# Unit phases of a diagonal state-space scan: a doubling ladder on VectorE, or products of two small tables on GpSimd

## The chip, the cores and the metric

The kernel runs on one core of a Trainium2 chip. Its time is the time of one execution in microseconds (us), as the device counts it; a kernel's figure is the median of several executions. The profile is of one such execution. Engines are named as in the profile: PE is TensorE's matmul, PEld its weight load, DVE is VectorE, ACT is ScalarE, POOL is GpSimd, and SP is SyncE, which only issues DMAs here. A semaphore orders the engines among each other; on one engine, instructions run strictly in the order of the program.

## The reference, cut to what matters

One decoder layer over 512 tokens of width 2048. An input projection gives 24 blocks of 128 channels: 8 go into a diagonal state-space group (S5), 16 into a gated causal convolution of 31 taps. Both are joined, go through an output projection and a layer norm, then through a mixture of 32 experts, and a last gated embedding.

```python
z = x @ w_in + b_in
lam_bar = exp(lam * exp(log_dt))              # complex, 64 groups x 64 states
bu = einsum('blgh,gph->blgp', u, b_bar)
states = scan(s[t] = lam_bar * s[t-1] + bu[t])
y = einsum('blgp,ghp->blgh', states, c).real + d_skip * u
...
h = conv31(v * sigmoid(g)); y_conv = silu(layer_norm(h))
y = concatenate([y_ssm, y_conv]) @ w_o + b_o
```

The kernel splits the 512 steps into 64 columns of 8 steps. Over the columns it needs a complex scan with the factor lam_bar^8. It takes the angle out: the input of column n is turned back by the unit phase exp(-i a n), a real scan with the modulus runs over the columns, and the result is turned forward by exp(i a n). So it needs, for each of the 64 groups and 64 states, cos(a n) and sin(a n) for n = 0 to 63. Those are the unit phases.

## The kernel before, in words

Stage 1 goes over the 24 blocks of the input projection in the order written in `order` (lines 268 and 594 to 629). A block is 48 matmuls of 128x512 into the bank `zp` (`mm3`, lines 99 to 102: each product is split in a high and a low part, three matmuls). Their weights come as `raw` over SP, ACT casts the high part `whi` (line 79), and DVE, for the last four blocks and for the GLU weights POOL, takes the low part `wlo` (line 80). Between the matmuls of later blocks stand the small matmuls of the state-space tiles: `x_mm` (L516), `y_mm` (L540 and L541), the transposes L466 and the kernel products L473 and L474.

For each of the 8 state-space blocks (tiles), `ssm_tables(ft)` makes what depends on parameters alone. On POOL: `bw` (L439 to L444) and the tables `wt` and `t1` (L452 to L454). On ACT: the copies `wx`, `kpad`, `mt`, and eight copies that spread the phases `cc` and `ss` into `pc` and `pz` (L495 to L498). `bw` has one buffer, so POOL's L439 of a tile waits until PE has read the tile before (L474); `cc` and `ss` have one buffer too, so they are written again only after ACT's eight copies. `ssm_tile` then does the scan on DVE: L525 to L534, with the scan itself at L529; its result `sc` goes to `y_mm`. `activate` takes the bank `yp` with an ACT copy (L548), sends it through DRAM, and DVE and ACT apply the skip and the GELU (L553 to L560); SP writes the result to `z_dram` (L561).

The phases are made by `phases(ft)`, once for two tiles: a ladder of six doublings, n = 1, 2, 4, 8, 16, 32, each of six DVE instructions (L412 to L417) on 128 x 8 x n elements, 36 instructions a call and four calls. POOL only sets the first element (L404, L405).

Each convolution channel block is 30 DVE instructions in a row (L236, "taps"), with the running sum in a PSUM bank `cps`; their result `acc` goes to `c_dram` over SP (L238). DVE has no other large work that is as free to wait: blocks 0 to 5 of the convolution end with the tap loop inside stage 1.

Stage 2 begins when all eight `z_dram` are back in SBUF as `zraw` (L608) and split into `zh` and `zl`: four blocks of GLU matmuls (192 of 128x512), then the output projection, first with the state-space half `y0`, later with the convolution half `y1`. Its DVE work is the last taps, the GLU gate (L717), the low parts `y0l`, and additions of the bias (L741). The mean over channels of the convolution is taken on PE by L686 and L687, after DVE's L677. Stage 3 routes the tokens and streams expert weights, stage 4 is the gated embedding.

The order on each engine isn't the order of the source: a scheduler plays the program through with its own estimate of durations and writes the engines' instructions in the order in which they would start. A change of one instruction's engine so moves others too.

Of the kernel before, what the change touches and what calls it, by code (L numbers as in the profile page):

```python
# [8 lines left out]
FT = mybir.dt.float32  # L9
# [3 lines left out]
OP = mybir.AluOpType  # L13
# [4 lines left out]
P = 128  # L18
# [4 lines left out]
NN = S // NB  # L23
# [31 lines left out]
def build(tc, I, out, dbg=None, stages=9):  # L55
    nc = tc.nc
    V = nc.vector
    A = nc.scalar
    G = nc.gpsimd
# [72 lines left out]
    def exp_parts(pool, x, shape, tag):  # L132
        def w(nm, dt=FT):
            return pool.tile(shape, dt, name=f"{tag}{nm}")
        xc, k, r, h, k2 = w("xc"), w("k"), w("r"), w("h"), w("k2")
        s = w("s", I32)
        V.tensor_scalar(xc, x, -87.0, 88.0, op0=OP.max, op1=OP.min)
        V.tensor_scalar(k, xc, LOG2E, MAGIC, op0=OP.mult, op1=OP.add)
        V.tensor_scalar(k, k, -MAGIC, None, op0=OP.add)
        V.scalar_tensor_tensor(r, k, -LN2H, xc, op0=OP.mult, op1=OP.add)  # L140
        V.scalar_tensor_tensor(r, k, -LN2L, r, op0=OP.mult, op1=OP.add)
        V.tensor_scalar(h, r, 1.0 / 5040, None, op0=OP.mult)
        for cf in (1.0 / 720, 1.0 / 120, 1.0 / 24, 1.0 / 6, 0.5, 1.0):
            V.scalar_tensor_tensor(h, h, cf, r, op0=OP.add, op1=OP.mult)
        V.tensor_scalar(k2, k, 127.0, 8388608.0, op0=OP.add, op1=OP.mult)
        V.tensor_copy(s, k2)
        return h, s.bitcast(FT)
# [96 lines left out]
    def bank(name, bufs=1):  # L244
        if name in bturn:

            n = bturn[name]
            bturn[name] += 1
            name, bufs = (("zp", 4) if n % 5 < 4 else ("xp", 1)) if name == "ops" else (("wps", "cps")[n % 2], 1)
        return psA.tile([P, 512], FT, name=name, tag=name, bufs=bufs)  # L250

    if True:
        with ExitStack() as s2:
            xpool = s2.enter_context(tc.tile_pool(reuse_waits="tile", name="xpool", bufs=1))
            vstk = ExitStack()
            tpool = vstk.enter_context(tc.tile_pool(reuse_waits="tile", name="tpool", bufs=1))
# [38 lines left out]
            spool = setup.enter_context(tc.tile_pool(reuse_waits="tile", name="spool", bufs=1))  # L295
# [10 lines left out]
            h, s2k = exp_parts(spool, ldt, [P, 1, NG], "edt")  # L306
# [13 lines left out]
            h, s2k = exp_parts(spool, er, [P, 2, NG], "eer")  # L320
# [67 lines left out]
                V.tensor_tensor(hi, hi, t4, op=OP.add)  # L388
            V.tensor_scalar(Li, Li, sig, None, op0=OP.mult)

            Cb = tpool.tile([P, 8, 4, 6], FT, name="Cb")
            Sb = tpool.tile([P, 8, 4, 6], FT, name="Sb")
            for dst, srct in ((Cb, cs), (Sb, sn)):
                for hf in range(2):
                    ph = slice(64 * hf, 64 * hf + 64)
                    V.tensor_copy(dst[ph].rearrange("p t g j -> p j t g"),
                                  srct[ph, 1:7].rearrange("p j (t u g) -> p j t u g", t=8, u=2)[:, :, :, hf])

            def phases(ft):

                cc = tpool.tile([P, 8, NN], FT, name="cc")
                ss = tpool.tile([P, 8, NN], FT, name="ss")
                tm = vpool.tile([P, 8, NN // 2], FT, name="tm", tag="xr", bufs=1)
                G.memset(cc[:, :, 0:1], 1.0)  # L404
                G.memset(ss[:, :, 0:1], 0.0)  # L405
                bases = [t[:, ft:ft + 2].rearrange("p t g j -> p (t g) j") for t in (Cb, Sb)]
                for j in range(6):
                    m = 1 << j
                    cb_, sb_ = (b[:, :, j:j + 1].broadcast_to([P, 8, m]) for b in bases)
                    t_ = tm[:, :, 0:m]  # L410
                    c0, c1, s0, s1_ = cc[:, :, 0:m], cc[:, :, m:2 * m], ss[:, :, 0:m], ss[:, :, m:2 * m]
                    V.tensor_tensor(c1, c0, cb_, op=OP.mult)  # L412
                    V.tensor_tensor(t_, s0, sb_, op=OP.mult)
                    V.tensor_tensor(c1, c1, t_, op=OP.subtract)
                    V.tensor_tensor(s1_, s0, cb_, op=OP.mult)
                    V.tensor_tensor(t_, c0, sb_, op=OP.mult)
                    V.tensor_tensor(s1_, s1_, t_, op=OP.add)  # L417
                return cc, ss

            cs_pair = []  # L420
            setup.close()
            vpool = vstk.enter_context(tc.tile_pool(reuse_waits="tile", name="vpool", bufs=2))
            E = G

            def ssm_tables(ft):
# [20 lines left out]
                big = tpool.tile([P, GT, CH, NB], FT, name="big")  # L446
# [23 lines left out]
                for g in range(GT):  # L470
                    j, c = g % 4, g // 4
# [15 lines left out]

                pc = vpool.tile([P, GT, NN], FT, name="pc", bufs=2)
                pz = vpool.tile([P, GT, NN], FT, name="pz", bufs=2)
                if ft % 2 == 0:  # L490
                    cs_pair[:] = phases(ft)
                cc, ss = (t[:, 4 * (ft % 2):4 * (ft % 2) + 4] for t in cs_pair)
                for hf in range(2):
                    src_, gh = slice(64 * hf, 64 * hf + 64), slice(4 * hf, 4 * hf + 4)
                    A.copy(pc[0:64, gh], cc[src_])  # L495
# [98 lines left out]
            for s_, f in enumerate(order):  # L594
# [18 lines left out]
                kind, j = f // 8, f % 8  # L613
                if s_ == 2:
                    tabs[0] = ssm_tables(0)
                if kind == 0:
                    u = vpool.tile([P, S], FT, name="u", bufs=3)
                    A.activation(u, ps, AF.Identity, bias=b_in[:, j:j + 1])
                    ssm_tile(j, u, tabs.pop(j))
                    if j < 7:  # L620
                        tabs[j + 1] = ssm_tables(j + 1)
                elif kind == 1:
                    gates[j] = ps
                else:
                    hcs.append(conv_gate(j, gates.pop(j), ps))
                    if 1 <= j < 7:
                        conv_taps(j - 1)
                    if j == 6:
                        conv_taps(6)
# [4 lines left out]
    if True:  # L634
# [59 lines left out]
        sh = [P, NT, P]  # L694
        rows = []
        for x, n in ((rs4, "sqs"), (d4, "near")):
            t = lp_.tile(sh, FT, name="diag", tag=n)
# [5 lines left out]
        sh_ = lp_.tile([P, S], FT, name="sh_")  # L703
        A.copy(sh_, ps)

        for q in range(4):
            hl = next(w_in)
            for f in range(2):
                wh, wl = hl[f]
                ps = bank("ops")  # L710
                for k in range(8):
                    sl = slice(k * P, (k + 1) * P)
                    mm3(ps, wh[:, sl], wl[:, sl], zh[:, k], zl[:, k], k == 0, k == 7)
                ft = 2 * q + f
# [66 lines left out]
        with ExitStack() as s3:  # L781
# [126 lines left out]
            def rt(name, *shape):  # L908
                return rp.tile([P, *shape], FT, name=name)
# [38 lines left out]
            cn, cc = bank("ops"), bank("ops")  # L948
# [25 lines left out]
            sv = rt("sv", 3, 2 * NT)  # L974
# [62 lines left out]
    if True:  # L1037
# [105 lines left out]
        for i, (width, members) in enumerate(GROUPS):  # L1143
# [16 lines left out]
            with tc.If(most > 0):  # L1160
                cv, cg = Carve(ob), Carve(gx)
                sv, place = cv.tile([P, 3, 2 * NT]), cv.tile([P, NP])
# [56 lines left out]
    with ExitStack() as s5:  # L1219
# [111 lines left out]
        for c in range(4):  # L1331
# [18 lines left out]
            for m in range(NT):  # L1350
# [14 lines left out]
                if c == 3:  # L1365
                    gate(m, c, ps[m], bpg)
                    mean, rstd = ln_stats(fh, st3[:, m], "s")
                    for q in range(2):
                        i = slice(q * 1024, (q + 1) * 1024)
# [67 lines left out]
```

## Time and profile before

| | us |
|---|---|
| median of 3 runs | 1529.64 (1523.28 to 1530.3) |
| the profiled execution | 1528.31 |
| its span, first to last instruction | 1526.6 |
| stage 1, to the first GLU matmul | 0 to 418.2 |
| GLU and output projection | 418 to about 700 |
| routing | about 700 to 785 |
| experts | 785 to about 1280 |
| gated embedding | to the end |

In the whole span PE is busy 83%, DVE 54%, ACT 24%, POOL 22%. The shares mean little for this change: in stage 1 DVE is busy nearly all the time, later hardly. In the expert stage the chain that ended last is nearly all DMA of expert weights, each piece a load of some 20 us. The stages follow each other: the expert weights that are routed can't be asked for before the routing is done.

### The profile page before, as it was taken

What the parts mean: (1) busy time and instruction counts of PE and PEld (TensorE: products, weight loads), DVE (VectorE), ACT (ScalarE), POOL (GpSimd) and SP (SyncE); (2) the same over time, 40 slices, a digit from 0 to 9 for tenths busy, and PEclk for the clock granted to TensorE, in tenths of its full rate; (3) what the DMA queues carried; (4) which work ended last, traced back from release to release, by engine and by line L of the source; (5) the groups of instructions that cost most, each with busy time, mean ns of one, the idle gap of its engine ahead of it and who ended that gap; (6) DMA issues with size and microseconds to landing.
All of it is one profiled execution on the core that took longest, in us unless ns stands there. A gap on an engine that the chain in (4) does not pass through costs nothing. (4 is left out here: it accounts for less than half of the span.)

```text
span 1526.6 us, 16736 instructions
## 1 busy us (share of the span) xinstructions
PE 1260.8 (83%) x6206; PEld 806.8 (53%) x6207; DVE 825.5 (54%) x1369; ACT 371.6 (24%) x558; POOL 332.8 (22%) x273
## 2 busy tenths in 40 slices
PE   6988989899489999997639898977776766489996
PEld 4766768777368788874313332312211211378884
DVE  7999999969998934375101111100000005976567
ACT  4332634454243613122000111100000003023210
POOL 0444435373283520000001111100000003710000
PEclk9989889999799999998669999998889887689998
DMA  6333434433723235123899999999999996326312
GB/s 227 109 99 116 132 112 136 123 113 110 273 102 123 77 114 200 58 81 151 344 407 387 420 412 420 421 417 417 416 410 410 420 398 245 117 109 228 120 60 117
DMA packets 97497, 349.21 MB, mean 229 GB/s; under 512 B 29688, under 2 KB 43256, under 8 KB 61824
## 3 DMA queue, kind: packets, MB, share of 16 engines
q1 hardware_dynamic: 50880, 303.08, 51.2%
q10 hardware_dynamic: 40912, 28.20, 6.3%
q0 software_dynamic: 5616, 16.79, 2.8%
q8 instruction: 51, 0.84, 0.2%
q14 instruction: 38, 0.31, 0.1%
HBM read 323.17 MB, written 35.34 MB: 235 GB/s over the span
## 5 line engine op out<-in xcount | busy, mean ns | idle before, releaser
L1093 PE MATMUL gu<-ring,xt 128*32 128x512 f32 (+2 forms) x1144 | 234.8, 676 | 54.3 <-DMA ring<-w_gu 54.2
L236 DVE SCALAR_TENSOR_TENSOR cps<-hc,wdw,cps 128x512 f32<-128x512 f32 x232 | 174.0, 750 | 3.2
L100 PE MATMUL zp<-xh,whi 128*128 128x512 f32 x384 | 157.7, 412 | 10.7 <-ACT whi L79 10.1
L79 ACT CAST whi<-raw 128x1024 fp32r<-128x1024 f32 x116 | 119.4, 1046 | 177.6 <-PE zp L102 60.0
L1093 PEld LDWEIGHTS gu<-ring,xt 128*32 128x32 f32 (+2 forms) x1144 | 58.8, 128 | 194.7 <-issue 102.9
L102 PE MATMUL zp<-xh,wlo 128*128 128x512 f32 x384 | 156.0, 406 | 3.1 <-DVE wlo L80 3.1
L101 PE MATMUL zp<-xl,whi 128*128 128x512 f32 x384 | 156.5, 408 | 1.6 <-DVE xl L80 1.6
L80 DVE TENSOR_TENSOR wlo<-raw,whi 128x1024 fp32r<-128x1024 f32 x90 | 119.3, 1336 | 59.8 <-ACT whi L79 58.8
L1099 DVE TENSOR_TENSOR act<-act,gu 128x256 f32<-128x256 f32 x13 | 5.5, 422 | 259.1 <-ACT act L1098 259.1
L1113 PE MATMUL dps<-ring,at 128*32 128x512 f32 (+2 forms) x568 | 116.7, 625 | 10.7 <-ACT at L1104 5.5
L1063 POOL DMA_INDIRECT y_dram<-ob,sl x26 | 25.6, 986 | 364.7 <-ACT ob L1115 355.5
L100 PE MATMUL fps<-whi,h2h 128*128 128x512 f32 x224 | 89.6, 401 | 1.0 <-ACT h2h L79 1.0
L102 PE MATMUL fps<-whi,h2l 128*128 128x512 f32 x224 | 89.7, 401 | 0.0
L100 PEld LDWEIGHTS zp<-xh,whi 128*128 128x128 f32 x384 | 75.2, 196 | 26.2 <-ACT whi L79 9.8
L101 PE MATMUL fps<-wlo,h2h 128*128 128x512 f32 x224 | 88.9, 398 | 0.0
L1078 DVE COPY xt<-xtp 128x512 f32<-128x512 f32 x26 | 18.0, 692 | 128.5 <-PE xtp L1073 128.5
L102 PEld LDWEIGHTS zp<-xh,wlo 128*128 128x128 f32 x384 | 75.2, 196 | 20.9 <-DVE wlo L80 4.3
L80 POOL TENSOR_TENSOR wlo<-raw,whi 128x1024 fp32r<-128x1024 f32 x26 | 68.0, 2621 | 81.1 <-ACT whi L79 72.6
L101 PEld LDWEIGHTS zp<-xl,whi 128*128 128x128 f32 x384 | 75.3, 196 | 17.4 <-DVE xl L80 2.0
L1115 DVE COPY ob<-dps 128x512 f32<-128x512 f32 x26 | 18.0, 692 | 103.5 <-PE dps L1113 103.5
L1113 PEld LDWEIGHTS dps<-ring,at 128*32 128x32 f32 (+2 forms) x568 | 31.5, 122 | 79.6 <-issue 57.7
L1073 PE MATMUL xtp<-ident,gx 128*128 128x128 f32 x208 | 35.9, 298 | 39.1 <-DMA gx<-h_dram,sl 29.7
(434 smaller groups left out, 2287.1 us busy)
## 6 DMA issues: line engine op xcount, KB each, us to landing
ring<-w_gu SPq DMA_DIRECT2D x114, 1024.0 KB, 20.9
ring<-w_dn SPq DMA_DIRECT2D x56, 1024.0 KB, 20.6
raw<-w_in SPq DMA_DIRECT2D x24, 1024.0 KB, 5.5
raw<-w_o SPq DMA_DIRECT2D x16, 1024.0 KB, 4.8
raw<-w_gu SPq DMA_DIRECT2D x14, 1024.0 KB, 19.0
raw<-w_pg SPq DMA_DIRECT2D x14, 1024.0 KB, 5.8
raw<-w_dn SPq DMA_DIRECT2D x8, 1024.0 KB, 23.9
raw<-y_dram SPq DMA_DIRECT2D x12, 512.0 KB, 6.8
```

Source lines behind the costliest of these rows:

```text
L79: A.copy(hi, src)
L80: eng.tensor_tensor(lo, src, hi.bitcast(FT), op=OP.subtract)
L100: T.matmul(ps, lh, rh, start=start, stop=False)
L101: T.matmul(ps, lh, rl, start=False, stop=False)
L102: T.matmul(ps, ll, rh, start=False, stop=stop)
L236: V.scalar_tensor_tensor(ps if k < 30 else acc, hc[:, k:k + S], wdw[:, ct, k:k + 1], ps, op0=OP.mult, op1=OP.add)
L1063: G.indirect_dma_start(out=y_dram[q], out_offset=bass.IndirectOffsetOnAxis(ap=isc, axis=0), in_=ob[:, q * 1024:(q + 1) * 1024], in_offset= ...
L1073: T.transpose(ps[:, kk * P:(kk + 1) * P], gx[:, k * P:(k + 1) * P], ident)
L1078: V.tensor_copy(o, ps)
L1093: T.matmul(gu[cols], xt[:, k, cols], raws[j][:, kk * 512:(kk + 1) * 512], start=k == 0, stop=k == KD - 1)
L1113: T.matmul(outs[c][cols], at[:, k, cols], raws[j][:, o:o + 512], start=k == 0, stop=k == 1)
L1115: (A.copy if c else V.tensor_copy)(ob[:, q * 1024 + c * 512:q * 1024 + (c + 1) * 512], outs[c])
```

## The change

`phases` goes. The table of powers is made once for all tiles on DVE: `tc_` and `ts_` hold cos and sin of 8 low powers (n = 0 to 7) and of 8 high ones (n = 0, 8, ..., 56), for all 32 rows of groups, by three doublings of six instructions each, 18 instructions in all. In each of the 8 tiles POOL then makes `cc` and `ss` as the product of high and low power: six instructions of 128 x 256 elements, with a piece of `big` as scratch. `cc` and `ss` now cover one tile instead of two, still with one buffer each.

```diff
@@ -388,36 +388,32 @@
                 V.tensor_tensor(hi, hi, t4, op=OP.add)
             V.tensor_scalar(Li, Li, sig, None, op0=OP.mult)
 
-            Cb = tpool.tile([P, 8, 4, 6], FT, name="Cb")
-            Sb = tpool.tile([P, 8, 4, 6], FT, name="Sb")
+            Cb = spool.tile([P, 8, 4, 6], FT, name="Cb")
+            Sb = spool.tile([P, 8, 4, 6], FT, name="Sb")
             for dst, srct in ((Cb, cs), (Sb, sn)):
                 for hf in range(2):
                     ph = slice(64 * hf, 64 * hf + 64)
                     V.tensor_copy(dst[ph].rearrange("p t g j -> p j t g"),
                                   srct[ph, 1:7].rearrange("p j (t u g) -> p j t u g", t=8, u=2)[:, :, :, hf])
 
-            def phases(ft):
-
-                cc = tpool.tile([P, 8, NN], FT, name="cc")
-                ss = tpool.tile([P, 8, NN], FT, name="ss")
-                tm = vpool.tile([P, 8, NN // 2], FT, name="tm", tag="xr", bufs=1)
-                G.memset(cc[:, :, 0:1], 1.0)
-                G.memset(ss[:, :, 0:1], 0.0)
-                bases = [t[:, ft:ft + 2].rearrange("p t g j -> p (t g) j") for t in (Cb, Sb)]
-                for j in range(6):
-                    m = 1 << j
-                    cb_, sb_ = (b[:, :, j:j + 1].broadcast_to([P, 8, m]) for b in bases)
-                    t_ = tm[:, :, 0:m]
-                    c0, c1, s0, s1_ = cc[:, :, 0:m], cc[:, :, m:2 * m], ss[:, :, 0:m], ss[:, :, m:2 * m]
-                    V.tensor_tensor(c1, c0, cb_, op=OP.mult)
-                    V.tensor_tensor(t_, s0, sb_, op=OP.mult)
-                    V.tensor_tensor(c1, c1, t_, op=OP.subtract)
-                    V.tensor_tensor(s1_, s0, cb_, op=OP.mult)
-                    V.tensor_tensor(t_, c0, sb_, op=OP.mult)
-                    V.tensor_tensor(s1_, s1_, t_, op=OP.add)
-                return cc, ss
-
-            cs_pair = []
+
+            tc_, ts_ = (tpool.tile([P, 2, 32, 8], FT, name=n) for n in ("tc_", "ts_"))
+            V.memset(tc_[:, :, :, 0:1], 1.0)
+            V.memset(ts_[:, :, :, 0:1], 0.0)
+            tm_ = spool.tile([P, 2, 32, 4], FT, name="tm_")
+            bases = [t.rearrange("p t g (a j) -> p a (t g) j", a=2) for t in (Cb, Sb)]
+            for j in range(3):
+                m = 1 << j
+                cb_, sb_ = (b[:, :, :, j:j + 1].broadcast_to([P, 2, 32, m]) for b in bases)
+                t_ = tm_[:, :, :, 0:m]
+                c0, c1, s0, s1_ = (t[:, :, :, a:a + m] for t in (tc_, ts_) for a in (0, m))
+                V.tensor_tensor(c1, c0, cb_, op=OP.mult)
+                V.tensor_tensor(t_, s0, sb_, op=OP.mult)
+                V.tensor_tensor(c1, c1, t_, op=OP.subtract)
+                V.tensor_tensor(s1_, s0, cb_, op=OP.mult)
+                V.tensor_tensor(t_, c0, sb_, op=OP.mult)
+                V.tensor_tensor(s1_, s1_, t_, op=OP.add)
+
             setup.close()
             vpool = vstk.enter_context(tc.tile_pool(reuse_waits="tile", name="vpool", bufs=2))
             E = G
@@ -487,9 +483,17 @@
 
                 pc = vpool.tile([P, GT, NN], FT, name="pc", bufs=2)
                 pz = vpool.tile([P, GT, NN], FT, name="pz", bufs=2)
-                if ft % 2 == 0:
-                    cs_pair[:] = phases(ft)
-                cc, ss = (t[:, 4 * (ft % 2):4 * (ft % 2) + 4] for t in cs_pair)
+                cc, ss = (tpool.tile([P, 4, NN], FT, name=n) for n in ("cc", "ss"))
+                sh = [P, 4, 8, 8]
+                cl, ch, sl, sh_ = (t[:, a, 4 * ft:4 * ft + 4].unsqueeze(3 if a else 2).broadcast_to(sh) for t in (tc_, ts_) for a in range(2))
+                cv, sv = (t.rearrange("p g (a b) -> p g a b", b=8) for t in (cc, ss))
+                tm = big.rearrange("p g h i -> p (g h i)")[:, 0:256].rearrange("p (g a b) -> p g a b", a=8, b=8)
+                E.tensor_tensor(cv, ch, cl, op=OP.mult)
+                E.tensor_tensor(tm, sh_, sl, op=OP.mult)
+                E.tensor_tensor(cv, cv, tm, op=OP.subtract)
+                E.tensor_tensor(sv, sh_, cl, op=OP.mult)
+                E.tensor_tensor(tm, ch, sl, op=OP.mult)
+                E.tensor_tensor(sv, sv, tm, op=OP.add)
                 for hf in range(2):
                     src_, gh = slice(64 * hf, 64 * hf + 64), slice(4 * hf, 4 * hf + 4)
                     A.copy(pc[0:64, gh], cc[src_])
```

The scheduler moves much else. Three places follow. The first is POOL from the end of tile 0's tables to the start of tile 1's. Before:

```order
L453 TENSOR_TENSOR big<-Li,cb 128x1024
L454 TENSOR_TENSOR t_510<-t_510,big 128x1024
L404 MEMSET cc 128x8
L569 MEMSET hc 128x30
L439 TENSOR_TENSOR bw<-ba,qr 128x8x16
```

and now:

```order
L449 TENSOR_TENSOR big<-Li,cb 128x1024
L450 TENSOR_TENSOR t_533<-t_533,big 128x1024
L492 TENSOR_TENSOR big<-ts__308 128x256
L493 TENSOR_TENSOR cc<-cc,big 128x256
L495 TENSOR_TENSOR big<-tc__307,ts__308 128x256
L496 TENSOR_TENSOR ss<-ss,big 128x256
L491 TENSOR_TENSOR cc<-tc__307 128x256
L494 TENSOR_TENSOR ss<-ts__308,tc__307 128x256
L573 MEMSET hc 128x30
L435 TENSOR_TENSOR bw<-ba,qr 128x8x16
```

The phases of a tile stand behind its tables, the first two instructions of the next tile's phases right behind them, and then `bw` of the next tile. L491 and L494 wait for ACT's copies of the tile before.

The second place is SP at the end of stage 1 (`z_dram_78` to `85` are the eight tiles' results, `c_dram_86` to `92` those of convolution blocks 0 to 6). Before:

```order
L75 DMA raw<-w_glu 128x2048
L561 DMA z_dram_85<-gl 128x512
L238 DMA c_dram_92<-acc 128x512
L608 DMA zraw<-z_dram_78 128x512
...
L608 DMA zraw<-z_dram_85 128x512
L611 DMA hcv<-c_dram_86 128x512
```

and now:

```order
L238 DMA c_dram_91<-acc 128x512
L565 DMA z_dram_85<-gl 128x512
L612 DMA zraw<-z_dram_78 128x512
...
L612 DMA zraw<-z_dram_85 128x512
L615 DMA hcv<-c_dram_86 128x512
...
L75 DMA raw<-w_o 128x2048
L238 DMA c_dram_92<-acc 128x512
L615 DMA hcv<-c_dram_92 128x512
```

The write of convolution block 6 stood ahead of the loads of `zraw`, and now stands behind them.

The third place is DVE at the same point. Before:

```order
L236 SCALAR_TENSOR_TENSOR cps<-hc,wdw,cps 128x512 x12
L236 SCALAR_TENSOR_TENSOR acc<-hc,wdw,cps 128x512
L234 TENSOR_SCALAR cps<-hc,wdw,bdw 128x512
L236 SCALAR_TENSOR_TENSOR cps<-hc,wdw,cps 128x512 x6
L80 TENSOR_TENSOR zl<-zraw,zh 128x512
```

and now:

```order
L236 SCALAR_TENSOR_TENSOR acc<-hc,wdw,cps 128x512
L562 TENSOR_TENSOR gl<-gl,yc 128x512
L234 TENSOR_SCALAR cps<-hc,wdw,bdw 128x512
L236 SCALAR_TENSOR_TENSOR cps<-hc,wdw,cps 128x512
L564 TENSOR_TENSOR gl<-yc,gl 128x512
L236 SCALAR_TENSOR_TENSOR cps<-hc,wdw,cps 128x512 x7
L80 TENSOR_TENSOR zl<-zraw,zh 128x512
```

The `acc` in the first piece is that of convolution block 6, in the second that of block 5: with the change, 8 taps of block 6 stand ahead of `zl`, and 22 of it and all 30 of block 7 behind it.

## Rows read from the trace of the kernel before

**Rows 1.** Windows: us, each engine's busy us (instructions), TensorE clock, DMA share, GB/s.

```profile
30.00:418.00 388.00, 332.09 (x1803) 272.28 (x1801) 367.36 (x541) 164.46 (x254) 170.72 (x135) 0.92 0.43 134
390.00:420.00 30.00, 8.39 (x33) 6.23 (x31) 27.55 (x39) 6.36 (x10) 5.15 (x5) 0.67 0.78 292
418.00:506.00 88.00, 83.43 (x350) 65.99 (x351) 81.72 (x115) 35.27 (x58) 51.50 (x29) 0.95 0.33 114
```

**Rows 2.** Waits of PE, 0 to 700 us: us in total, times, longest.

```profile
PE zp L100 <- ACT zh L79: 21.6, 1, 21.6
PE yp L540 <- ACT yb L548: 12.4, 3, 7.4
PE xp L516 <- ACT whi L79: 7.5, 1, 7.5
PE yp L541 <- DVE sc L534: 5.9, 2, 5.5
PE wps L466 <- POOL wt L454: 4.9, 1, 4.9
```

**Rows 3.** Timeline of SP, end of stage 1: start us, us, engine, line, what.

```profile
404.24 0.33 SPq L561 DMA_DIRECT2D z_dram<-gl  x1
414.40 0.33 SPq L238 DMA_DIRECT2D c_dram<-acc  x1
414.77 3.94 SPq L608 DMA_DIRECT2D zraw<-z_dram  x8
```

**Rows 4.** Timeline of PE: last tile's L541, end of stage 1, one in stage 2.

```profile
386.31 0.39 PE L541 MATMUL yp<-sc,t 128*128 128x63 f32 x2
...
396.21 0.40 PE L102 MATMUL zp<-xh,wlo 128*128 128x512 f32 x1
...
505.69 0.39 PE L101 MATMUL zp<-wlo,y0h 128*128 128x512 f32 x1
```

**Rows 5.** DVE groups, 0 to 418 us: count | busy us, mean ns | idle before.

```profile
L414 DVE TENSOR_TENSOR cc<-cc,tm 128x8 f32<-128x8 f32 (+5 forms) x24 | 17.4, 723 | 0.0
L413 DVE TENSOR_TENSOR tm<-ss,Sb 128x8 f32<-128x8 f32 (+5 forms) x24 | 16.3, 677 | 0.1
L416 DVE TENSOR_TENSOR tm<-cc,Sb 128x8 f32<-128x8 f32 (+5 forms) x24 | 14.7, 613 | 0.2
L412 DVE TENSOR_TENSOR cc<-cc,Cb 128x8 f32<-128x8 f32 (+5 forms) x24 | 11.0, 460 | 0.0
L417 DVE TENSOR_TENSOR ss<-ss,tm 128x8 f32<-128x8 f32 (+5 forms) x24 | 10.1, 419 | 0.0
L415 DVE TENSOR_TENSOR ss<-ss,Cb 128x8 f32<-128x8 f32 (+5 forms) x24 | 7.8, 323 | 0.0
L383 DVE TENSOR_TENSOR Lr<-Lr 128x64 f32<-128x64 f32 (+2 forms) x3 | 1.0, 337 | 0.0
```

**Rows 6.** Timeline of DVE and of POOL, 285 to 288 us.

```profile
285.72 1.70 DVE L413 TENSOR_TENSOR tm<-ss,Sb 128x8 f32<-128x8 f32 x1
287.34 0.74 DVE L236 SCALAR_TENSOR_TENSOR cps<-hc,wdw,cps 128x512 f32<-128x512 f32 x1
...
285.37 2.03 POOL L452 TENSOR_TENSOR wt<-Lr,bw 128x1024 f32<-128x1024 f32 x1
```

**Rows 7.** POOL groups of the nearest sizes, 0 to 560 us.

```profile
L443 POOL TENSOR_TENSOR sm<-ba,qi 128x128 f32<-128x128 f32 x8 | 4.8, 601 | 0.4
L670 POOL TENSOR_TENSOR near<-near,hcv 128x512 f32<-128x512 f32 x4 | 5.8, 1458 | 0.3
```

**Rows 8.** Timeline of ACT: one of the eight copies.

```profile
154.06 0.41 ACT L498 ACTIVATE pz<-ss 64x256 f32<-64x256 f32 x1
```

**Rows 9.** Waits of POOL, 0 to 560 us: us in total, times, longest.

```profile
POOL bw L439 <- PE wps L474: 45.1, 6, 15.9
POOL cc L404 <- ACT pc L496: 23.0, 1, 23.0
```

**Rows 10.** DVE groups, 418 to 506 us.

```profile
L766 DVE TENSOR_TENSOR hcv<-hcv,cps 128x512 f32<-128x512 f32 x8 | 4.9, 676 | 0.0
```

## The prediction, made before the changed kernel ran

> **What bounds the kernel now.** I read the busy shares by slice first: DVE is full in the first third of the span and nearly empty in the middle, and the removed work lies in that first third. So stage 1 is looked at alone. Its windows [rows 1] show DVE busy 367 of the 388 us from 30 to 418, 95%, and POOL 171, under half; PE looks busy at 332, but matmuls overlap, and its waits tell more. In stage 1 four groups hold it up, together 12.4 + 7.5 + 5.9 + 4.9 = 30.7 us, and one wait of 21.6 us ends the stage [rows 2]. Behind such waits the clock falls: the window's mean granted clock is 0.92, so 0.08 x 388 = 31 us of full speed are missing [rows 1]. Some 10 of them fall into the last wait (0.33 x 30 in the window 390 to 420 [rows 1]); of the rest I put 5 inside the other waits and 16 on matmuls that ran at the lower level. So PE loses 31 + 16 + 22 = 69 us to the other engines in stage 1, and could have reached the GLU at about 418 - 69 = 349.
>
> DVE's figure is alike. Almost without a gap it has done 418 us of its order when the stage ends. Both engines so have about the same bound, once DVE has less to do. PE's waits are mostly for DVE, directly or in a chain: ACT takes its instructions in order and waits for DVE, and PE for ACT.
>
> The last wait is worth a look [rows 3, 4]. PE ends its last block at 396.2 + 0.4. The last tile's result goes out at 404.2, and its reload is the next thing that PE needs; but SP has the write of convolution block 6 in between, whose taps DVE finishes only at 414.4. The reload starts at 414.8, PE at 418.2.
>
> **The change, part by part.**
>
> Removed from DVE: six groups of 24 instructions, 17.4 + 16.3 + 14.7 + 11.0 + 10.1 + 7.8 = 77.3 us [rows 5]. That is much for so little data, and rows 6 show why: an instruction on 128x8 elements takes 1.70 us, from 285.72 to 287.42, and POOL's L452 runs from 285.37 to 287.40. A DVE instruction with both inputs in SBUF waits until POOL's is through. A tap right behind it, with one input in PSUM, takes its 0.74 us [rows 6].
>
> The Trainium skill, SBUF — State Buffer, section "SBUF: two separate sides", states that as a rule: one port pair is an exclusive lock between a DVE instruction with two SBUF inputs and a GpSimd instruction, the later one blocks for the whole of the other. The trace agrees (1.70 us). Perfetto Trace Analysis, section "Optimizing Scalar/DVE Operations", in the Trainium skill draws the conclusion that moving work between the two might not help. It is the third rival below.
>
> Added on DVE: 18 instructions on up to 128x256 elements at the 0.337 us of L383 [rows 5], 6 us, early, where DVE also waits for loads. Bounds: 3 and 12 us.
>
> Added on POOL: 48 instructions on 128x256. Between 0.60 us for 128x128 and 1.46 for 128x512 [rows 7] I take 0.8, as a straight line gives: 38 us, and keep 29 and 70 as ends. What covers them: POOL waits 45.1 us, six times, for PE before it may write `bw` again [rows 9], 7.5 us a tile. Four of the six stand just ahead of that wait, and so do the next tile's first two. The latter wait in their turn for ACT's copies; I put 1.7 us on that (four copies are left after `ss`, 0.41 each [rows 8]). 6 x 0.8 + 1.7 = 6.5, under 7.5, though not by much. The wait of 23.0 us [rows 9] was the same kind: POOL stood before a memset of `cc`, until ACT had the phases from DVE, and the tables of tile 1, for which PE waits 4.9 us, were behind it. POOL now makes these phases itself right after tile 0's tables, and I expect this wait to go.
>
> The price on DVE: 38 us more of POOL in which its remaining two-input instructions may be caught. Bounds 0 and 38. The taps aren't caught and fill about half of DVE's time; I take 5. So DVE is relieved by 77 - 6 - 5 = 66 us in stage 1.
>
> What that gives. If PE lost no time, the GLU would start at 349 plus 3 or so, that is 66 earlier; DVE, at 418 - 66, and with 22 taps x 0.74 = 16 us [rows 6] moved behind the stage, would be ready at 336. I don't take it whole: some of PE's waits are for transfers and for ACT's own order, and two engines that are both near their bound hold each other up. Of the 31 + 16 us I count half, 24 us. The last wait I count as gone but for 3: SP no longer has block 6 in front of the reload, and the y matmuls of the last tile stand 2.2 blocks (some 25 us) before the end of the projection, where 22 us are needed from them to the GLU (386.3 to 404.2, and from 414.8 to 418.2 for the reload [rows 3, 4]). That is 19 us. Together 43.
>
> What is late next. The 22 taps, 16 us, now lie behind `zl`, before the subtraction for which L687 waits and partly before `y0l` of the last GLU block, which PE needs. DVE was busy 81.7 of 88 us from 418 to 506 [rows 1]. Of that some 14 us (L766 with 4.9 [rows 10], and the small steps of the norm and some additions) now come later, and 16 come in: 84 us of work, 87 to 92 us with its gaps. PE's matching point, the 311th large matmul of stage 2, was at 505.7 [rows 4], 87.5 us after 418.2. So PE gives back 0 to 5 us there and once more clock; I take 4. From there on PE is busy without a gap until about 700, the order of the later engines is nearly the old one, and routing and experts follow: what is left is kept to the end.
>
> Sum: 43 - 4 = 39 us. Against the profiled execution 1528.3 - 39 = 1489; that lies 1.3 us under the median of the runs, so 1490 for a median.
>
> **The rivals.**
>
> *All waits go.* DVE was the one cause. For it: its 95%, and that each of the four waits leads back to a late DVE or POOL result. Against: two bounds that meet at 336 to 352. Gain 66 - 4 = 62: 1468 as a median, like the times below.
>
> *DVE only filled its time.* The taps may wait for long, so less DVE work only brings them forward, and PE's waits, of which two name ACT, stay. Only the reload's 19 us are won, less 4: 1515.
>
> *The lock takes half of it back.* All 38 us of POOL's new time fall on DVE, and the relief is 77 - 6 - 38 = 33 us. Then half of the 24 us is won, 12, and the 19; behind the stage DVE is later by some 5 more: 12 + 19 - 9 = 22 us, 1508. For it: a mean of 723 ns in L414 [rows 5]. Against: much of stage 1's DVE time is taps, and POOL's new instructions are short.
>
> *GpSimd becomes the bound: slower.* The loop PE L474, POOL `bw` and tables, PE transposes has 7.5 us of slack a tile [rows 9]. The six instructions and the wait for ACT fill it when one takes 0.97 us; at the upper end, 1.46, it is 8.8 + 1.7 - 7.5 = 3.0 us a tile, and with ACT's eight copies serial (3.3 instead of 1.7) 4.6. Over seven tiles 32 us, against 19 won at the reload, and 4 given back: 17 us slower, 1547. For it: single buffers of `cc`, `ss` and `bw`. Against: the straight line between rows 7.
>
> **How the numbers follow.** Forecast 0.50 (its own range 1477 to 1502), all waits 0.15, DVE a filler 0.15, the lock 0.13, GpSimd 0.07. A measurement of this kernel can tell about 0.5%, 7.6 us: faster is below 1522. The first four lie there, though the second and third rival reach over with some 0.07 of their share; so faster 0.86, the same 0.08, slower 0.06. The range from 1466 to 1519 leaves out the upper tail and a little of the lowest case.
>
> **What would show it.** Right: no DVE groups of 24 on `cc` and `ss`; 48 POOL instructions at 0.7 to 0.9 us; the first GLU matmul at 365 to 385; no wait of over 5 us ahead of it; POOL's wait for L470 shorter than 45 us but not gone; a new wait of PE, of 5 to 20 us, for `y0l` or for the subtraction in stage 2. Wrong: POOL instructions over 1 us and PE waiting for `wt` in each tile, which is the last rival; the first GLU matmul later than 400, with DVE idle, the second; DVE still full and its remaining tensor_tensor means up by a half, the third; or stage 2 giving back more than 15 us.

## The result, and the profile after

The changed kernel takes 1482.9 us as the median of four runs (1481.08 to 1484.66), the kernel before 1528.67 beside it (1523.28 to 1530.3). The ratio is 0.971, with a 95% interval from 0.969 to 0.973. The profiled execution took 1484.66 us, its span 1482.9, against 1526.6 before.

The stages come first, with the same columns as [rows 1]: the stretch, busy time and number of instructions of PE, PEld, DVE, ACT and POOL, the granted clock, the DMA share.

```profile
30.00:373.00 343.00, 326.77 (x1803) 270.07 (x1802) 312.93 (x396) 166.84 (x259) 218.20 (x179) 0.96 0.46 141
373.00:461.00 88.00, 83.90 (x356) 67.28 (x355) 83.08 (x124) 28.70 (x47) 53.56 (x27) 0.95 0.45 165
```

Stage 1 ends at 373 instead of 418. In it PE is without work for 343 - 327 = 16 us, before for 388 - 332 = 56 [rows 1]; the clock has gone from 0.92 to 0.96, and the same matmuls are busy 5 us less. So 45 = 40 + 5, and of the 40 the last wait of before is 21.6. DVE is still busy 91% of the time: it didn't get empty, it got through.

The waits of PE up to 700 us, those of stage 1 and then the two of stage 2 that stand nearest to the forecast's (us in total, times, longest):

```profile
PE yp L545 <- DVE sc L538: 8.1, 5, 4.0
PE yp L544 <- ACT mt L482: 4.5, 2, 2.5
PE wps L469 <- ACT wx L463: 1.9, 2, 1.3
PE wps L462 <- POOL wt L450: 1.3, 1, 1.3
PE xp L101 <- DVE wlo L80: 3.1, 1, 3.1
PE zp L100 <- DVE tt L752: 1.0, 1, 1.0
```

One wait of the kernel before in stage 2, at the mean over the channels, has no counterpart now:

```profile
PE yp L687 <- DVE hcv L677: 4.0, 1, 4.0
```

The four of stage 1 make 15.8 us, where four made 30.7, and the wait of 21.6 us at its end [rows 2] is gone. How wholly it is gone, SP and PE show (start, duration, engine, line, what):

```profile
360.75 0.33 SPq L565 DMA_DIRECT2D z_dram<-gl  x1
361.16 4.00 SPq L612 DMA_DIRECT2D zraw<-z_dram  x8
...
397.14 0.33 SPq L238 DMA_DIRECT2D c_dram<-acc  x1
```

```profile
373.17 0.40 PE L102 MATMUL zp<-xh,wlo 128*128 128x512 f32 x1
373.40 0.40 PE L100 MATMUL zp<-zh,whi 128*128 128x512 f32 x1
```

The reload goes out 0.4 us after the last result, 12 us before PE needs it, and the first GLU matmul follows the last block without a gap; before, SP stood with the write of block 6 in between [rows 3, 4]. From there to the end of the span it is 1109.5 us, before 1526.6 - 418.2 = 1108.4: of the 44.8 us that stage 1 won, 1.1 are given back.

Three waits of GpSimd in its loop over the tiles (to 560 us) and three of the six new groups (count | busy us, mean ns | idle before):

```profile
POOL bw L435 <- PE wps L470: 22.9, 6, 6.5
POOL ss L494 <- ACT pz L502: 10.2, 7, 3.0
POOL cc L491 <- ACT pc L500: 4.8, 4, 1.8
```

```profile
L496 POOL TENSOR_TENSOR ss<-ss,big 128x256 f32<-128x256 f32 x8 | 10.4, 1294 | 0.5
L492 POOL TENSOR_TENSOR big<-ts__308 128x256 f32<-128x256 f32 x8 | 8.1, 1008 | 0.2
L493 POOL TENSOR_TENSOR cc<-cc,big 128x256 f32<-128x256 f32 x8 | 7.1, 891 | 0.6
```

All six groups make 50.3 us. The wait for PE has halved from 45.1 [rows 9]: 3.7 us a tile of the slack are used up.

On DVE the ladder's 77.3 us [rows 5] have become 18 table instructions of 0.34 to 0.37 us, 6.3 us. What stayed on DVE takes longer. Groups of stage 1 from 30 us, first of before, then of after:

```profile
L80 DVE TENSOR_TENSOR wlo<-raw,whi 128x1024 fp32r<-128x1024 f32 x36 | 48.2, 1349 | 0.6 <-ACT whi L79 0.6
L527 DVE TENSOR_TENSOR xr<-xr,xs 128x512 f32<-128x512 f32 x8 | 8.7, 1081 | 0.0
L532 DVE TENSOR_TENSOR sc<-sc,pc 128x512 f32<-128x512 f32 x8 | 5.8, 722 | 0.0
```

```profile
L80 DVE TENSOR_TENSOR wlo<-raw,whi 128x1024 fp32r<-128x1024 f32 x36 | 53.1, 1482 | 1.3 <-ACT whi L79 1.3
L531 DVE TENSOR_TENSOR xr<-xr,xs 128x512 f32<-128x512 f32 x8 | 12.5, 1558 | 0.1
L536 DVE TENSOR_TENSOR sc<-sc,pc 128x512 f32<-128x512 f32 x8 | 10.4, 1294 | 1.4 <-ACT xs L535 1.4
```

The ten groups of scan and activation together went from 83.6 to 93.9 us, the 36 `wlo` from 48.2 to 53.1, 15 us in all. Not all of them grew: the scan itself went from 15.6 to 11.1. Rows of the new products beside DVE's instructions (start and duration):

```profile
81.49 1.23 DVE L574 SCALAR_TENSOR_TENSOR hc<-zp,b_in,sg 128x512 f32<-128x512 f32 x1
82.13 0.74 POOL L493 TENSOR_TENSOR cc<-cc,big 128x256 f32<-128x256 f32 x1
...
119.47 0.62 POOL L491 TENSOR_TENSOR cc<-tc__307 128x256 f32<-128x256 f32 x1
119.50 1.67 DVE L80 TENSOR_TENSOR wlo<-raw,whi 128x1024 fp32r<-128x1024 f32 x1
...
277.23 1.83 POOL L496 TENSOR_TENSOR ss<-ss,big 128x256 f32<-128x256 f32 x1
277.24 1.22 DVE L80 TENSOR_TENSOR wlo<-raw,whi 128x1024 fp32r<-128x1024 f32 x1
```

Beside DVE instructions with one input in PSUM (L574, then taps) an instruction of the products takes 0.74 us. Where a DVE instruction with two inputs in SBUF runs beside it, either of the two can be held up: at 277.23 the product takes 1.83 and ends 0.6 us after DVE's 1.22, at 119.5 the product takes its 0.62 and the `wlo` 1.67 instead of 1.22. The Trainium skill, SBUF — State Buffer, section "SBUF: two separate sides", says that whichever of the two starts first has the ports for its whole instruction and the other is blocked. The trace agrees that one of the two runs undisturbed and the other doesn't; which of them was first, starts that lie 0.01 us apart in the profile (277.23 and 277.24) don't tell. How much of the 15 us is the price of these products is another question: e9 below shows that a part of it, at the least 6 us, comes without them.

### The profile page after: what moved, and what is told of

Its sections match the earlier page's. It is cut to its first block, busy times and chain, and to the rows that moved or that the text cites. A ratio compares the mean times of both kernels' runs of the same rounds, so it can differ in the third digit from the quotient of the medians.

```text
span 1482.9 us, 16658 instructions
## 1 busy us (share of the span) xinstructions
PE 1253.2 (85%) x6206; PEld 803.9 (54%) x6207; DVE 777.4 (52%) x1245; ACT 371.2 (25%) x558; POOL 384.5 (26%) x313
## 4 chain that ended last, share of the span: by engine, by line
PE 22%; DMA 21%; DVE 5%; issue 1%; ACT 1%; POOL 0%; DVEq 0%; SPq 0%; ACTq 0%; POOLq 0%
DMA ring<-w_gu 12%; PE gu L1097 6%; DMA ring<-w_dn 6%; PE dps L1117 3%; PE fps L102 3%; PE fps L101 3%; PE fps L100 3%; DMA raw<-w_gu 3%; PE xtp L1077 1%; DMA gx<-h_dram,sl 1%; DVE tt L181 1%; DVE tt L180 1%; DVE lny L170 1%; PE h2p L101 0%; PE h2p L102 0%
## 5 line engine op out<-in xcount | busy, mean ns | idle before, releaser
L80 DVE TENSOR_TENSOR wlo<-raw,whi 128x1024 fp32r<-128x1024 f32 x90 | 124.5, 1393 | 56.4 <-ACT whi L79 55.5
L1117 PE MATMUL dps<-ring,at 128*32 128x512 f32 (+2 forms) x568 | 113.6, 606 | 11.8 <-DMA ring<-w_dn 6.2
L80 POOL TENSOR_TENSOR wlo<-raw,whi 128x1024 fp32r<-128x1024 f32 x26 | 71.0, 2731 | 86.3 <-ACT whi L79 73.8
```

What stands on the lines that cost most here:

```text
L80: eng.tensor_tensor(lo, src, hi.bitcast(FT), op=OP.subtract)
L1117: T.matmul(outs[c][cols], at[:, k, cols], raws[j][:, o:o + 512], start=k == 0, stop=k == 1)
```

## The experiments

The theory: VectorE's load in stage 1 is the cause, about half of its relief reaches TensorE, and the reload of the eight results comes early besides. Rivals: the reload's place alone; the move to GpSimd without the table; the lock between the two engines eats much of it. Times are medians; "before" is the kernel before, measured beside it. The GLU column is the start of the first GLU matmul in the profiled execution.

| run | GLU | us | before | ratio (95%) |
|---|---|---|---|---|
| before | 418.2 | 1528.7 | | |
| changed | 373.4 | 1482.9 | 1528.7 | 0.971 (0.969 to 0.973) |
| products on VectorE (e1) | 377.7 | 1491.1 | 1525.5 | 0.976 (0.974 to 0.978) |
| ladder on GpSimd (e2) | 385.8 | 1500.6 | 1525.5 | 0.982 (0.980 to 0.984) |
| products once (e3) | 365.1 | 1482.4 | 1525.5 | 0.972 (0.969 to 0.975) |
| products twice (e4) | 387.6 | 1497.6 | 1525.5 | 0.981 (0.979 to 0.983) |
| before, no write of block 6 (e5) | 410.8 | 1521.9 | 1524.9 | 0.998 (0.997 to 0.999) |
| changed, reload behind (e6) | 387.9 | 1499.0 | 1524.9 | 0.984 (0.981 to 0.986) |
| before, one ladder (e7) | 380.2 | 1492.4 | 1524.9 | 0.979 (0.977 to 0.982) |
| products once, again (e8) | 373.1 | 1484.5 | 1524.9 | 0.972 (0.970 to 0.975) |
| before, no ladder (e9) | 367.5 | 1482.5 | 1526.2 | 0.971 (0.969 to 0.973) |
| changed, memset on VectorE (e10) | 369.0 | 1480.9 | 1526.2 | 0.970 (0.968 to 0.972) |
| changed again (e11) | 368.9 | 1482.5 | 1526.2 | 0.971 (0.968 to 0.973) |

**The products on VectorE (e1).** The table is kept, the move undone.

```diff
-                E.tensor_tensor(cv, ch, cl, op=OP.mult)
+                V.tensor_tensor(cv, ch, cl, op=OP.mult)
...
```

> The changed kernel with the six product instructions of each tile on VectorE instead of GpSimd. VectorE gets 48 instructions of 128x256 back, by an estimate 0.35 to 0.7 us each (17 to 34 us), and loses some 12 us of waiting for GpSimd's products. Theory (VectorE's load decides, half of it reaches TensorE): 5 to 20 us more of VectorE, so 1486 to 1498, with the GLU starting some 5 to 12 us later than 373. Rival A (only the reload of the eight results ahead of convolution block 6 counted; that order is kept here): 1483 within 4. Rival B (the move to GpSimd is the gain, the table none): VectorE full again, over 1510.

Measured: 1491.1, 8 us over the changed kernel, the theory's middle, with the GLU 4 us later, not 5 to 12. The 48 instructions took 22.8 us on DVE, 0.41 to 0.43 each in four of the six groups. So the table alone, wherever its products are made, brings 34 of the 44 to 46 us; rivals A and B both fall. Its window shows something else:

```profile
30.00:377.00 347.00, 336.71 (x1813) 281.02 (x1813) 335.44 (x441) 166.22 (x258) 170.65 (x128) 0.93 0.44 136
```

PE is without work for 10 us here, less than in the changed kernel. The loss stands in the clock, 0.93 against 0.96, and in 10 us more of busy matmuls.

**The ladder on GpSimd (e2).** Before, all `V.tensor_tensor` of `phases` as `G.tensor_tensor`: the move without the table.

> The kernel before with its whole ladder (36 instructions a call, four calls) on GpSimd instead of VectorE: the move without the table. VectorE is relieved by 77 us as before the price of the lock; GpSimd gets 144 small instructions, some 18 us a call by the durations of its 128x128 and 128x256 instructions, in one lump for every second tile. Theory (VectorE's load decides, and GpSimd has 7.5 us of slack a tile): most of the gain stays, less some 5 to 8 us in each of three lumps: 1490 to 1510. Rival (GpSimd's loop becomes the bound without the table): TensorE waits for wt in every second tile, 1525 or more.

Measured: 1500.6, in the theory's range. GpSimd spends 73.4 us on the 144 instructions, the worst group at 578 ns:

```profile
L417 POOL TENSOR_TENSOR ss<-ss,tm 128x8 f32<-128x8 f32 (+5 forms) x24 | 13.9, 578 | 0.1
```

Some of DVE's relief then goes into waits of PE for the tables `wt` (4.3 us) and for their copies `wx` (5.6 us). The move alone brings 25 us.

**The products twice (e4), and once (e3, e8).** Twelve instructions a tile, or six in all:

```diff
+                E.tensor_tensor(cv, ch, cl, op=OP.mult)
...
+                E.tensor_tensor(sv, sv, tm, op=OP.add)
                 E.tensor_tensor(cv, ch, cl, op=OP.mult)
...
```

```diff
+                if ft == 0:
...
+                    cs_pair[:] = cc, ss
+                cc, ss = cs_pair
```

> The changed kernel with the six products made twice in each tile: GpSimd has 50 us more, 6.3 us a tile, where its wait for TensorE ahead of bw is now 22.9 us in six waits and that for the phase buffers 15 us in eleven. Theory (a loop PE, bw, tables, PE with its slack nearly used): the loop is 2 to 4 us a tile over, and VectorE some 12 us later through the lock: 1493 to 1512, TensorE waiting for wt. Rival (GpSimd's products are off the path, and a second set is too): 1483 to 1489.

> The changed kernel with the six products made in tile 0 alone and read by all tiles (the later tiles' phases are left out, so the result is not the reference's). GpSimd loses 42 instructions, 44 us, and VectorE's remaining two-input instructions lose the waits for them, some 13 us. Theory (stage 1 is near TensorE's own bound: 16 us idle and some 14 us of clock are left ahead of the GLU): 3 to 10 us faster than the changed kernel, 1473 to 1480. Rival A (the lock took half of the gain back): 20 us or more, 1463 or less. Rival B (GpSimd's new work is wholly covered): 1483 within 3.

> The changed kernel with the products made in tile 0 alone, once more (the later tiles' phases are left out, so the result is not the reference's): its profile had the GLU 8 us earlier than the changed kernel and ended 9 us earlier, but its four times spread from 1475.6 to 1488.2. Theory (stage 1 is shorter by 8 us each time, what varies lies behind stage 2): GLU start within 2 us of 365.1, and times that spread again from about 1475 to 1488 with the difference in the routing or expert stage. Rival (stage 1 varies itself): a GLU start other than 365 where the time is over 1483.

Twice costs 15 us: 1497.6, the GLU 14 later. The loop is then over its slack: GpSimd's wait for L470 ahead of `bw` is gone, and PE waits more, 10.4 us for the scan and 7.6 for `wx`. DVE's ten groups and the `wlo` take 12.6 us more than in the changed kernel (159.6 against 147.0), so the loop and DVE's delay come together here. The expectation named `wt` for this wait; it is `wx`, ACT's copy right behind it.

```profile
PE yp L551 <- DVE sc L544: 10.4, 5, 4.4
...
PE wps L469 <- ACT wx L463: 7.6, 2, 5.4
```

Once costs as much as in each tile: 1482.4 and 1484.5, rival B of e3. The first 50 us of GpSimd's new work are covered, the second 50 are not. The first profile of this kernel promised 9 us all the same, and the second did not, so I compared the two, stretch by stretch. By 310 us e8 is 8 matmuls behind, by 340 us 51, so most of the difference lies between 310 and 340. Windows of e3 and of e8, then PE's wait for the scan in each between 300 and 330:

```profile
310.00:325.00 15.00, 13.55 (x103) 11.67 (x102) 13.98 (x17) 3.40 (x6) 4.40 (x2) 0.89 0.44 133
325.00:340.00 15.00, 15.00 (x84) 12.93 (x83) 14.68 (x20) 9.31 (x11) 7.71 (x3) 1.00 0.41 123
```

```profile
310.00:325.00 15.00, 11.91 (x78) 10.18 (x77) 14.03 (x15) 4.74 (x8) 4.80 (x2) 0.70 0.38 115
325.00:340.00 15.00, 15.00 (x66) 12.67 (x65) 9.79 (x12) 5.82 (x6) 3.96 (x2) 0.84 0.30 87
```

```profile
PE yp L550 <- DVE sc L543: 1.5, 1, 1.5
```

```profile
PE yp L550 <- DVE sc L543: 3.1, 1, 3.1
```

One wait that is 1.6 us longer, then a clock of 0.70 instead of 0.89 and of 0.84 instead of 1.00, and 43 matmuls fewer in 30 us. That stage 1 is shorter each time (the theory of e8) is wrong: its end moves by 8 us between executions of one kernel. A GLU start from a single profile is good to some 8 us, a median of times to some 3.

**The reload's place (e5, e6).** In the kernel before, block 6 leaves its result in SBUF, and SyncE has no write of it; in the changed kernel, the reload is forced behind block 6's last tap.

```diff
-                    for k in range(7):
+                    for k in range(6):
                         nc.sync.dma_start(hcv[:, k], c_dram[k])
+                    conv_taps(6, hcv[:, 6])
...
-                    if j == 6:
-                        conv_taps(6)
```

```diff
+                    acc6 = conv_taps(6)
+                    V.tensor_copy(zraw[:, :, 0:1], acc6[:, 0:8].unsqueeze(2))
                     for k in range(8):
                         nc.sync.dma_start(zraw[:, k], z_dram[k])
```

> The kernel before, in which the taps of convolution block 6 leave their result in SBUF (in hcv, as block 7 does), so that no write of block 6 stands ahead of the reload of the eight results on SyncE. VectorE's order is nearly the old one: all of block 6 and the first four taps of block 7 are still ahead of the first zl. Theory A (the last wait is SyncE's order, as the forecast put it): the reload goes out at about 405 instead of 414.8 and the 19 us of the last wait are won without anything else: GLU start at 408 or less, 1506 to 1513. Theory B (the last wait is VectorE's lateness: zl stands behind the same taps, which end at 414): the first GLU matmuls start at about 408 and then wait for zl; nothing is won, 1521 to 1530.

> The changed kernel with the reload of the eight results forced behind the last tap of convolution block 6 (VectorE copies eight columns of that result into zraw, which the reload then overwrites), as it stood before the change. 22 taps, 16 us, then lie ahead of the reload. Theory (the place of the reload counts in full): the reload starts at 378 to 383 instead of 361, the GLU at 388 to 395, and nearly all of it stays to the end: 1497 to 1505. Rival (the taps must be done anyway before stage 2 can end, so it is given back there): 1483 to 1490.

e5 wins 3 us (ratio 0.998, interval 0.997 to 0.999), where the theory of the forecast wanted 19. Its rows of SP, DVE and PE in order of time:

```profile
399.85 9.46 DVE L236 SCALAR_TENSOR_TENSOR cps<-hc,wdw,cps 128x512 f32<-128x512 f32 x12
399.96 0.33 SPq L561 DMA_DIRECT2D z_dram<-gl  x1
400.34 10.87 SPq L608 DMA_DIRECT2D zraw<-z_dram  x8
...
413.22 1.29 DVE L80 TENSOR_TENSOR zl<-zraw,zh 128x512 fp32r<-128x512 f32 x2
```

```profile
410.78 1.22 PE L100 MATMUL zp<-zh,whi 128*128 128x512 f32 x2 [17.27 <-ACT zh L79]
```

The reload does go out 14 us earlier. But DVE is in block 6's taps until 410 and reaches the first `zl` only at 413.2 (before: 419.9), and PE needs `zl` for the second matmul of each product. So 7 us were the most to be had. The transfer takes more of it: its first piece lands 9.7 us after its issue, not 3.4 as before; the loads of `tt` (4 x 1 MB) were issued 5 to 7 us ahead of it, in the kernel before 16 to 18, and one of `w_glu` (1 MB) 1.4 us ahead, before 11.6. Theory B is right as to the taps; that `zh` too was late makes the run no clean measure of it.

e6 is cleaner. Its SP row and its wait:

```profile
382.58 3.96 SPq L615 DMA_DIRECT2D zraw<-z_dram  x8
```

```profile
PE zp L100 <- ACT zh L79: 11.0, 1, 11.0
```

With 22 taps ahead of the reload the GLU starts 14.5 us later, and the kernel takes 1499.0, 16 us more. The same tap work costs 16 us ahead of the reload and next to nothing behind it.

**The ladder once, and not at all (e7, e9).** The kernel before, with GpSimd given nothing new: the phases of the first two tiles read by all (58 us off DVE), or no ladder at all (77 us off).

```diff
-                if ft % 2 == 0:
+                if ft == 0:
                     cs_pair[:] = phases(ft)
```

> The kernel before with the ladder called once, for the first two tiles, and its phases read by all tiles (the other phases are left out, so the result is not the reference's). VectorE loses 108 of 144 ladder instructions, some 58 us, and GpSimd gains nothing but is spared its waits for the phase buffers. It gives VectorE about the relief that the change does (77 less 7 for the tables and 9 to 15 of waiting for GpSimd). Theory (VectorE's relief is the cause of the whole gain): GLU start at 365 to 378, 1474 to 1488. Rival (the new place of the phases on GpSimd, right behind the tables and ahead of bw, is part of it): GLU start over 390, 1500 or more.

> The kernel before without its ladder: cos is set to 1 and sin to 0 once (the phases are left out, so the result is not the reference's). VectorE loses all 77 us of the ladder, that of the first call (19 us, between 60 and 100 us) among it; GpSimd gets no products. In the run with one ladder the first 36 instructions were still there, and TensorE still waited 4.8 us at 108 us for the tables of tile 1, because GpSimd stood before the memset of hc until VectorE's last tap of convolution block 0 at 95. Theory (VectorE's relief alone gives the whole gain, and the first ladder's place matters): that wait is gone or under 2 us, GLU start 362 to 375, 1473 to 1486. Rival (GpSimd's new order of the phases is needed for part of the gain): the wait at tile 1 stays, GLU start 378 or later, 1488 or more.

e7 gives 32 us: 1492.4, 4 us outside the theory's range and 8 short of the rival's. What lacks is lost early: PE still waits 4.8 us at 108 us for the tables of tile 1. Three rows of GpSimd, from before, e7 and the changed kernel (idle time ahead in brackets), show what it stood before:

```profile
94.73 0.11 POOL L404 MEMSET cc<- 128x8 f32 x1 [22.99 <-ACT pc L496]
```

```profile
95.28 0.12 POOL L569 MEMSET hc<- 128x30 f32 x1 [22.52 <-DVE acc L236]
```

```profile
90.23 0.12 POOL L573 MEMSET hc<- 128x30 f32 x1 [2.91 <-DVE acc L236]
```

Take the wait for `cc` away, and the memset of `hc` behind it waits just as long, for DVE's last tap of block 0, which the ladder of the first call holds up. e9 drops that ladder too, with `cc` set to 1 and `ss` to 0. The last tap then ends at 82 instead of 95, the wait at tile 1 goes, the GLU starts at 367.5, and the time is 1482.5, that of the changed kernel beside it. So taking the ladder off DVE makes the whole gain; that GpSimd does the products adds nothing and, in the end, costs nothing. With the ladder go the waits for its results, that of GpSimd (23.0 us) and those of ACT, here its longest for a result of the ladder:

```profile
ACT pc L495 <- DVE cc L414: 13.6, 2, 8.2
```

That row is of the kernel before. No run keeps the ladder's load without these waits, so what share each has stays open.

e9 also tells what the products cost DVE. Two of the groups that grew, in e9, where GpSimd makes no product at all:

```profile
L516 DVE TENSOR_TENSOR xr<-xr,xs 128x512 f32<-128x512 f32 x8 | 12.8, 1598 | 0.0
L521 DVE TENSOR_TENSOR sc<-sc,pc 128x512 f32<-128x512 f32 x8 | 7.9, 986 | 3.1 <-ACT xs L520 3.1
```

The ten groups and the `wlo` take 143.6 us here, 147.0 in the changed kernel, 131.8 before, and 138.4 and 139.3 with the products made once (e3, e8). So 3 to 9 of the 15 us can be put down to the products; the other 6 to 12 come without them, and no run shows why.

**The memset on VectorE (e10), and the changed kernel again (e11).**

```diff
-                G.memset(hc[:, 0:30], 0.0)
+                V.memset(hc[:, 0:30], 0.0)
```

> The changed kernel with the memset of hc (30 columns, eight times) on VectorE instead of GpSimd, so that GpSimd's tables no longer queue behind VectorE's taps. GpSimd's waits for acc are 4.2 us there, two times, and TensorE's only wait for wt is 1.3 us. Theory (GpSimd's loop still sets a little of stage 1): 0 to 4 us faster, 1479 to 1483. Rival (not on the path): 1483 within 3. If the waits it moves let the clock fall once less, up to 8 us faster.

> The changed kernel once more, beside the runs of this call, to see how far its GLU start and its time move between executions: the run with the products made once had its GLU at 365.1 and at 373.1 in two profiles. If the clock after small waits makes that difference, this kernel too shows a GLU start between 365 and 380 and a time between 1475 and 1488.

1480.9 against 1482.5: the intervals (0.968 to 0.972 and 0.968 to 0.973) overlap, so no gain is shown. The changed kernel's two profiles have the GLU at 373.4 and 368.9, and its nine times run from 1478.5 to 1485.0, as expected.

## Why the prediction was right, step by step

It said 1490; 1482.9 lies in its own range, 7 us below.

- *Half of the waits.* Right, nearly to the microsecond: 30.7 us of PE's waits became 15.8, and all of PE's idle time in stage 1 without the last wait went from 34 to 16. Of the 16 us that it put on matmuls at the lower clock, 5 went, not 8. But the half was a guess that no row stood behind; that it fits so closely is luck.
- *The last wait, 19 us.* It went wholly, 21.6 us. The size is right, the reason was half: the working named SyncE's order alone. e5 shows that this order brings 3 us while DVE is late, e6 that it costs 16 where DVE is not. Both had to go, and DVE's relief did both: in every run above with a relieved DVE but e6, which forbids it, the scheduler's order has the reload first.
- *DVE's relief, 66 us.* It was 77.3 - 6.3 - 15.2 = 56. The 15.2 that the remaining work grew by stand where the forecast had 5 for the lock; but only 3 to 9 of them are the products' (e9, e3, e8). The lock's price was so about right, and a growth that comes without the products was left out. It did no harm: e9, with 77.3 - 11.8 = 65.5 us of relief, is no faster. PE's waits there are for `wx`, `mt` and `sc`, 14.8 us together, nearly as many as in the changed kernel.
- *GpSimd's products, 38 us.* 50.3, or 1.05 us each, not 0.8. The straight line was also drawn wrong: between the two sizes [rows 7] it gives 0.89 us, 43 in all. An undisturbed instruction takes 0.62 to 0.74; what came on top is the lock, which I had priced on DVE's side only. With 1.05 the working's own sum for the loop, 6 x 1.05 + 1.7 = 8.0 us a tile, is over the slack of 7.5, and the products should have held PE up. Instead 3.8 us a tile are left. That the slack held is luck as far as this sum goes; beside it GpSimd's wait for DVE's taps ahead of `hc` fell from 17.6 to 4.2 us, and the wait of 23.0 went, but no run separates what made the room. e4 shows the point from which it doesn't last.
- *The wait of 23.0 us gone.* Right for the changed kernel. For the reason, see e7: the wait for `cc` covered another, for DVE, of the same length.
- *Given back in stage 2, 4 us, with a new wait of 5 to 20.* Wrong, and the step that failed: it was 1.1 us to the end of the span, and the nearest new waits are 3.1 and 1.0. Against them a wait of the kernel before is gone, 4.0 us at the very subtraction (L687 for L677) that was to be late. The count of DVE's work was good (84 us forecast, 83.1 in the window of 88), but it assumed that what is late on DVE there is late on PE, and PE ran beside it, busy 83.9 of the 88 us.

Of the rivals, *all waits go* fails by the 15.8 us left; *DVE only filled its time* by e7 and e9; *the lock takes half of it back* by e3 and e8, where GpSimd has nearly none of the products and the kernel is no faster. Its sign was half there, though: L527 (now L531) went up by 44% and L532 (now L536) by 79%, though part of that comes without the products (e9). The Trainium skill, Perfetto Trace Analysis, section "Optimizing Scalar/DVE Operations", warns that moving work between the two engines might not help. Here it did: 8 us for the products (e1) and 25 for the whole ladder (e2). *GpSimd becomes the bound* needs twice the work (e4), and even the whole ladder there (e2) stays 25 us ahead of the kernel before.

What stays open: how much of a microsecond's wait the clock adds. e3 against e8 suggests that it is much; e1, with fewer us of waits than the changed kernel and a lower clock, shows that the sum of the waits doesn't tell it. No run varied it on purpose.

## What to carry to other kernels

Ask which engine the *chain* of waits leads back to, not which one a row names: here a POOL and an SP row (`cc`, the write of block 6) both stood for a late VectorE. Taking the write away alone (e5) moved the wait to the next in line, and with the wait for `cc` gone but the first ladder kept (e7), `hc` waited just as long. Work that shares an engine with a queue of patient instructions is worth removing for what it lets the scheduler put first. And give the helper engine work up to its measured slack per tile: the first 50 us on GpSimd were free, the next 50 cost 15.

## What the runs showed of the hardware that I had not expected

The hold between VectorE and GpSimd works both ways: a GpSimd product of 0.74 us takes 1.83 beside a `wlo` of 1.22, and beside a product of 0.62 a `wlo` takes 1.67. A wait of PE seems to cost more than its length: in two executions of one program, with 1.5 against 3.1 us the granted clock was 0.89 against 0.70 in the same 15 us (means between the two levels of 1.2 and 2.4 GHz) and 1.00 against 0.84 in the next 15, and the stage ended 8 us later. And a load of 256 KB, issued 5 us behind 4 MB of others and 1.4 us behind one more MB, took 9.7 us to land, not 3.4.
